# Moving four pieces of work in a two-layer hybrid backbone, and ordering the whole program by a timeline

## The chip, the core and the metric

The kernel runs on one core of a Trainium2 chip. The core has a matrix engine (TensorE, PE in the rows), a vector engine (VectorE, DVE), a scalar engine (ScalarE, ACT), a general engine (GpSimd, POOL) and a queue that issues transfers (SyncE, SP). Each engine works through its own list of instructions in the order in which it was written; the lists meet only through waits on each other and on transfers (DMA). The metric is the time of one execution on the device, in microseconds (us).

## The reference

Two layers act on 1024 latent tokens and 256 context tokens of width 1024, all in fp32. Each layer is

```
h   = modulate(rms_norm(x), shift, scale)
aq,ak,av, bq,bk,bv, cx,cg = split(h @ W_in)       # three head groups
ya  = differential_attention(aq, ak, av)          # 4 heads, two softmax maps each
yb  = window_attention(bq, bk, bv, sink)          # 6 heads, window 128
yc  = bidirectional_RG_LRU(cx) * gelu(cg)         # width 384
x   = x + gate * (concat(ya, yb, yc) @ W_out)
h   = modulate(rms_norm(x), shift, scale)
x   = x + gate * (gelu-gated dwconv MLP(h) @ W_down)   # D_FF = 2816
```

The LRU part runs, for each of three groups of 128 channels and for both directions, a four-tap convolution along the tokens, two gate products with a block-diagonal matrix, a few pointwise functions (tanh, exp, sqrt) and a linear recurrence over all 1280 tokens; both directions are added and multiplied with the gated branch. Only the latent tokens of the last layer are the output.

## The kernel before, in words

A product in fp32 is made of three fast matmuls: each operand is split into a high part (`hi`, a copy on ACT, L184) and a low part (`lo`, a subtraction on DVE or POOL, L187), and high times high, high times low and low times high are added up in one bank of PE's accumulator memory. So every operand of a product has passed ACT and then DVE or POOL before PE can use it.

A layer has three phases. `phase_a` makes the projections of all three head groups, in three rounds j = 0, 1, 2. In each it makes query and key tiles (qkv_ps, with norm and rotation on DVE and POOL, transposed through PE as qk_t) or value tiles, and one third of the LRU: cx_ps, then in `lru` for each direction the convolution (L562, L569), the gates (gate_ps, L578, L579), exp, tanh and sqrt (L583, L584, L587), the pointwise products (L585, L588 on DVE, L586, L590 on POOL) and the recurrence as two scans (L593, L594 or L597, L599), and then in `lru_gate` the sum of both directions (L608), gelu on cg_ps (L614) and their product (L618). `phase_b` is the two attentions (sw for window, da for differential). `phase_c` is the output projection, the second norm, the feed-forward up (`up`, u_ps) and down (`down_steps`, d_ps and dc_ps).

The up products go by a scheme with fewer products: sums of quarters of the operands (s1 to s4, made in `norm_ops`, L1250 to L1264) take the place of some quarters. A product runs over four parts kk of its operand, each a high and a low tile (s_x, s_z). The down products work likewise, in steps: `prep` makes the sums of a product (d_s, d_t on POOL, L1342) and their splits (d_ah, d_al, d_b), and `split_ctx` splits the context operand (four pairs of 128x256, the low parts on POOL). The last two of the 22 slices of the down product are done apart, by `down` (L1735 to L1737), with operands from `load_u` in the last layer. In layer 0 this remainder is run by `tail`, in front of the `phase_a` of layer 1: it reads the residual (xt) back from memory, where `down_steps` stored it (xp), adds its products and makes the norm. This is called the seam. `weights` loads and splits the two weight tiles (w) that it needs.

The program falls into basic blocks: `phase_a` of layer 0, then `phase_b` and `phase_c` of layer 0, then the seam with `phase_a` of layer 1, then the rest of layer 1. Each engine ends a block's list before it begins the next one's. Within a block a scheduler puts each engine's list in order, by a model of when each instruction could start, and keeps dependences; only the seam block was ordered with the finer model, that follows a simulated timeline.

Of the kernel before, what the change touches and what calls it, by code (L numbers as in the profile page):

```python
# [11 lines left out]
F32 = mybir.dt.float32  # L12
F32R = mybir.dt.float32r
AF = mybir.ActivationFunctionType
ALU = mybir.AluOpType
# [155 lines left out]
class Build:  # L171
# [9 lines left out]


    def hi(self, out, in_):
        self.nc.scalar.activation(out, in_, AF.Copy)  # L184

    def lo(self, out, in_, hi, eng=None):
        (eng or self.nc.vector).tensor_tensor(out, in_, hi.bitcast(F32), ALU.subtract)  # L187

    def weight(self, src, n=1024):
        nc = self.nc  # L190
# [988 lines left out]
    def norm_ops(self, xt, am, bm, accs, f_tile, bank, ops, early, outs):  # L1179
# [13 lines left out]
        def unit(name, t, c=0):  # L1193
            p = t[:, c:c + 512], t[:, c + 512:c + 1024]
            ops[name].append(p)
            return p

        def split(p, v, eng):
            self.hi(p[0], v)
            self.lo(p[1], v, p[0], eng)  # L1200
# [51 lines left out]
        for kk in range(4):  # L1252
            s3 = v21[kk]
            nc.vector.tensor_tensor(s3, v11[kk], s3, ALU.subtract)
            split(unit("s3", (wa, wb)[kk // 2], 1024 * (kk % 2)), s3, nc.vector)
        ops["s2"].append(None)
        ops["s4"].append(None)
        for kk in range(4):
# [20 lines left out]
    def down_steps(self, xt, f_tile, bank):  # L1279
# [165 lines left out]
        load_ctx(0)  # L1445
        prep(0)
        prep(1)
        split_ctx()
        if steps > 1:
            load_ctx(1)  # L1450
        g = 0
        for s in range(steps):
            mine = [p for t, p in seq if t == s]
            for i, p in enumerate(mine):
                prep(g + 2)
                g += 1
                if p != "c":
                    product(s, p)
                if not self.last:

                    for q in {1: ("p1",), len(mine) - 1: ("c",)}.get(i, ()) + ((p,) if p in ("p2", "p3") else ()):
                        context(s, q)
                if s + 1 == steps:
                    for n in {"p2": ("x12",), "p5": ("x22",), "p7": ("x21",)}.get(p, ()):
                        spread(n)
                    for n in {"p2": ("x11",), "p7": ("x22",), "p3": ("x12",), "p4": ("x21",)}.get(p, ()):
                        store(n)
            if s + 1 < steps:
                split_ctx()
                if s + 2 < steps:  # L1470
                    load_ctx(s + 2)
# [3 lines left out]
    def phase_c(self):  # L1475
# [3 lines left out]
        with ExitStack() as st:  # L1479
# [65 lines left out]

            def product(ps, w, a, new, wts):
                (wh, wl), aa = wts[w], ops[a]
                for kk in range(4):
                    s = slice(P * kk, P * kk + P)
                    h, lo = aa[kk]  # L1550
                    nc.tensor.matmul(ps, wh[:, s], h, start=new and kk == 0, stop=False, skip_group_check=not new)  # L1551
                    nc.tensor.matmul(ps, wh[:, s], lo, start=False, stop=False, skip_group_check=not new)  # L1552
                    nc.tensor.matmul(ps, wl[:, s], h, start=False, stop=kk == 3, skip_group_check=not new)  # L1553

            def context(ps, w, new, wts):
                hh, hl = hc
# [151 lines left out]
            def load_u(f):  # L1708
                h, lo = self.h_tile("uh"), self.h_tile("ul")
                nc.sync.dma_start(lo[:, :n_tok].bitcast(F32), self.ud[f][:, :n_tok])  # L1710
                self.hi(h[:, :n_tok], lo[:, :n_tok].bitcast(F32))
                self.lo(lo[:, :n_tok], lo[:, :n_tok].bitcast(F32), h[:, :n_tok])
                return h, lo

            def down(fs, us, ds, end=False):
# [34 lines left out]
            if self.last:  # L1750
                ds = weights()
                down([NF - 2, NF - 1], [load_u(f) for f in (NF - 2, NF - 1)], ds)
            else:
                us = []
                for f in (NF - 2, NF - 1):
                    h, lo = f_tile("uh", F32R), f_tile("ul", F32R)
                    nc.sync.dma_start(lo.bitcast(F32), self.ud[f])
                    self.hi(h, lo.bitcast(F32))
                    self.lo(lo, lo.bitcast(F32), h)
                    us.append((h, lo))  # L1760
                stack = st.pop_all()

                def tail():
                    mods, self.mods = self.mods, self.modl[l]
                    ds = weights()
                    for j in range(KC):
                        xt[j] = self.x_tile(f"xt{j}") if j < KC - 1 else self.z_tile("xt7")[:, :T]
                    for o, n in CH:
                        for j in range(KC):
                            nc.sync.dma_start(xt[j][:, o:o + n], self.xp[j][:, o:o + n])  # L1770
                    down([NF - 2, NF - 1], us, ds, True)
                    self.mods = mods
                    stack.close()
                    del self.s5

                self.tail = tail
                return
# [26 lines left out]
```

## Time and profile before

| what | value |
|---|---|
| three timed runs | 3067.39, 3073.74, 3075.61 us; median 3073.74 |
| profiled execution | 3074.54 us, span 3072.8 us, mean granted clock 0.972 |
| PE, matmuls | 2836.2 us busy, 92% of the span |
| PE, weight loads | 2308.8 us, 75% |
| DVE | 2070.9 us, 67% |
| POOL | 1520.2 us, 49% |
| ACT | 1468.6 us, 48% |
| transfers | 349.25 MB, 114 GB/s in the mean |

The span runs from the first to the last instruction of the trace; 1.74 us of the execution lie outside. PE is busy nine tenths of the span, so the mean says little: a stage in which PE never stops and a stage in which it waits for an operand stand side by side. The rows below are read by stage. "Idle before" with an arrow says what ended the idle time of that instruction's engine.

### The profile page before, as it was taken

The numbers are of one execution on the slowest core, as the hardware profiler recorded it, in microseconds if no ns is written. First come the engines' busy times: TensorE is split into PE (matmuls) and PEld (weight loads), VectorE is DVE, ScalarE is ACT, GpSimd is POOL, SyncE is SP. The second block draws the span as 40 slices with busy tenths as digits, with TensorE's granted clock in tenths as the row PEclk, the third lists the DMA queues.
The fourth block names the chain that finished last, engine by engine and source line by source line (L and its number), as shares of the span: only waits on it lengthen the run. The fifth ranks groups of instructions, "written<-read, shape, count | busy, mean of one in ns | idle before, by whom it ended". The sixth has DMA issues, their size and how long they took to land. (4 is left out here: it accounts for less than half of the span.)

```text
span 3072.8 us, 40965 instructions
## 1 busy us (share of the span) xinstructions
PE 2836.2 (92%) x15146; PEld 2308.8 (75%) x15146; DVE 2070.9 (67%) x2879; ACT 1468.6 (48%) x2450; POOL 1520.2 (49%) x1011
## 2 busy tenths in 40 slices
PE   6999898999899999998988899898999799999898
PEld 4798665678688888886877788666777678887776
DVE  6956656884854444457887985757885755556997
ACT  5544467784443433342332554567883444444331
POOL 4746412323554444448561765512323576665971
PEclk9999999999899999998999999999999999999999
DMA  7232627664122111143215331545533122224322
GB/s 254 83 85 82 173 61 248 185 196 172 38 81 76 67 68 67 67 182 113 83 56 192 112 109 52 145 109 168 130 121 131 55 89 83 83 83 158 123 83 83
DMA packets 208280, 349.25 MB, mean 114 GB/s; under 512 B 32720, under 2 KB 112336, under 8 KB 208080
## 3 DMA queue, kind: packets, MB, share of 16 engines
q1 hardware_dynamic: 203472, 331.69, 33.3%
q0 software_dynamic: 4608, 14.95, 2.2%
q8 instruction: 119, 1.95, 0.3%
q14 instruction: 81, 0.66, 0.1%
HBM read 257.19 MB, written 89.39 MB: 113 GB/s over the span
## 5 line engine op out<-in xcount | busy, mean ns | idle before, releaser
L184 ACT ACTIVATE w_r<-w_raw 128x512 fp32r<-128x512 f32 x338 | 212.7, 631 | 451.4 <-PE u_ps L1552 279.7
L1524 POOL TENSOR_TENSOR w_raw<-w_raw 128x512 f32<-128x512 f32 x176 | 249.9, 1425 | 229.3 <-DVE w_r L187 108.5
L187 DVE TENSOR_TENSOR w_r<-w_raw,w_r 128x512 fp32r<-128x512 f32 x206 | 151.3, 737 | 250.2 <-ACT w_r L184 250.1
L1551 PE MATMUL u_ps<-a,w_r 128*128 128x512 f32 x704 | 278.6, 396 | 5.1 <-DVE vb L1639 4.0
L1552 PE MATMUL u_ps<-a,w_r 128*128 128x512 f32 x704 | 277.5, 394 | 1.4 <-DVE a L187 1.2
L1553 PE MATMUL u_ps<-a,w_r 128*128 128x512 f32 x704 | 276.3, 392 | 0.0
L187 POOL TENSOR_TENSOR w_r<-w_raw,w_r 128x512 fp32r<-128x512 f32 x132 | 190.2, 1441 | 122.7 <-ACT w_r L184 117.5
L1403 PE MATMUL d_ps<-d_ah,d_b 128*128 128x512 f32 x560 | 225.2, 403 | 22.5 <-DVE xd L1380 12.3
L1404 PE MATMUL d_ps<-d_al,d_b 128*128 128x512 f32 x560 | 223.9, 400 | 6.2 <-DVE d_al L187 6.2
L946 DVE TENSOR_REDUCE da_sm<-da_s 128x1 f32<-128x1280 f32 (+1 forms) x144 | 194.9, 1367 | 43.6 <-PE da_s L936 42.7
L1405 PE MATMUL d_ps<-d_ah,d_b 128*128 128x512 f32 x560 | 223.3, 399 | 0.6 <-DVE d_b L187 0.6
L187 POOL TENSOR_TENSOR w<-raw,w 128x1024 fp32r<-128x1024 f32 (+2 forms) x62 | 141.1, 2283 | 144.1 <-ACT w L184 135.1
L953 ACT ACTIVATE da_e<-da_s,da_sm 128x1280 f32<-128x1280 f32 (+1 forms) x144 | 177.6, 1235 | 22.9 <-DVE da_sm L946 21.2
L1551 PEld LDWEIGHTS u_ps<-a,w_r 128*128 128x128 f32 x704 | 133.9, 190 | 34.6 <-DVE vb L1639 5.5
L1090 POOL TENSOR_TENSOR oy_x<-oy_x,oy_z 128x426 f32<-128x426 f32 (+3 forms) x48 | 52.1, 1086 | 216.3 <-ACT oy_z L1088 193.7
L1552 PEld LDWEIGHTS u_ps<-a,w_r 128*128 128x128 f32 x704 | 133.9, 190 | 29.5 <-DVE a L187 2.1
L1553 PEld LDWEIGHTS u_ps<-a,w_r 128*128 128x128 f32 x704 | 133.6, 190 | 28.8
L1380 DVE SCALAR_TENSOR_TENSOR xd<-d_ps,mods,xd 128x512 f32<-128x512 f32 x200 | 141.0, 739 | 19.7 <-PE d_ps L1405 19.4
L1403 PEld LDWEIGHTS d_ps<-d_ah,d_b 128*128 128x128 f32 x560 | 108.7, 194 | 48.3 <-DVE xd L1380 10.0
L936 PE MATMUL da_s<-dak,daq 96*128 96x512 f32 (+1 forms) x400 | 123.0, 395 | 13.7 <-ACT da_e L953 13.3
L1639 DVE TENSOR_TENSOR vb<-u_ps,vb 128x512 f32<-128x512 f32 x96 | 66.0, 688 | 99.2 <-PE u_ps L1553 90.5
L1551 PE MATMUL u_ps<-s_x,w_r 128*128 128x512 f32 x308 | 122.0, 396 | 10.1 <-ACT s_x L184 10.1
(349 smaller groups left out, 8616.3 us busy)
## 6 DMA issues: line engine op xcount, KB each, us to landing
wmod<-in_wmod SPq DMA_DIRECT2D x96, 512.0 KB, 6.5
w_raw<-in_wu SPq DMA_DIRECT2D x44, 1024.0 KB, 5.4
d_w<-in_wd SPq DMA_DIRECT2D x40, 512.0 KB, 3.9
d_a<-ud SPq DMA_DIRECT2D x40, 512.0 KB, 4.6
ud<-conv SPq DMA_DIRECT2D x22, 640.0 KB, 2.9
ud<-conv SPq DMA_DIRECT2D x22, 512.0 KB, 2.6
raw<-in_wg SPq DMA_DIRECT2D x16, 512.0 KB, 4.1
dak<-qk_da POOLq DMA_DIRECT2D x48, 160.0 KB, 4.6
```

What stands on the lines that cost most here:

```text
L184: self.nc.scalar.activation(out, in_, AF.Copy)
L187: (eng or self.nc.vector).tensor_tensor(out, in_, hi.bitcast(F32), ALU.subtract)
L946: nc.vector.tensor_reduce(st["sm"][:, mi:mi + 1], st["s"][mi][:, :b["nkc"]], AX.X, ALU.max, negate=True)
L953: nc.scalar.activation(e[:, :nkc], st["s"][mi][:, :nkc], AF.Exp, bias=st["sm"][:, mi:mi + 1], accum_out=b["s0"][:, ti, u["hd"], mi:mi + 1])
L1380: nc.vector.scalar_tensor_tensor(x, ps, gate, x, ALU.mult, ALU.add)
L1403: nc.tensor.matmul(ps, bh[:, w], ah[:, m], start=on is None and k == 0, stop=False, **kw)
L1404: nc.tensor.matmul(ps, bh[:, w], al[:, m], start=False, stop=False, **kw)
L1405: nc.tensor.matmul(ps, bl[:, w], ah[:, m], start=False, stop=k == 1, **kw)
L1524: sub = lambda o, a, b, op=ALU.subtract: nc.gpsimd.tensor_tensor(o, a, b, op)
L1551: nc.tensor.matmul(ps, wh[:, s], h, start=new and kk == 0, stop=False, skip_group_check=not new)
L1552: nc.tensor.matmul(ps, wh[:, s], lo, start=False, stop=False, skip_group_check=not new)
L1553: nc.tensor.matmul(ps, wl[:, s], h, start=False, stop=kk == 3, skip_group_check=not new)
```

## The change

Four pieces of work are moved, and the whole program is ordered by the finer model, not only the seam block.

- Seam weights: `ds = weights()`, two weight loads and their splits, leaves `tail` and is called at the end of `phase_c` of layer 0, so it lies one block earlier.
- s2 parts: in the last layer the sums s2 and s4 and their splits are written in another order, the part kk = 0 late; `product` takes s2 and s4 in the order kk = 1, 2, 3, 0 in both layers.
- Last splits: the two splits of `load_u` are kept in the order of the program, so they are not put ahead of what is written before them.
- Context split: in the first step of layer 0's down products, `split_ctx` and the next load of the context come after the sums of the third product, not after the second.

```diff
+        if self.last:
+            ...
+            s2(0)
+            s4(0)
+            s2(1)
+            put("s2", 1, nc.vector)
+            s2(2)
+            put("s2", 2, nc.vector)
+            s4(1)
+            s2(3)
+            put("s2", 3, nc.vector)
+            s4(2)
+            put("s2", 0, nc.vector)
+            s4(3)
+            put("s4", 1, nc.gpsimd)
+            put("s4", 2, nc.vector)
+            put("s4", 3, nc.gpsimd)
+            put("s4", 0, nc.vector, self.z_tile("s_z", F32R))
+            return None
...
         prep(1)
-        split_ctx()
-        if steps > 1:
-            load_ctx(1)
         g = 0
         for s in range(steps):
...
                 prep(g + 2)
+                if g == 0:
+                    split_ctx()
+                    if steps > 1:
+                        load_ctx(1)
...
-                for kk in range(4):
+                for i in range(4):
+                    kk = (i + 1) % 4 if a in ("s2", "s4") else i
...
-                self.hi(h[:, :n_tok], lo[:, :n_tok].bitcast(F32))
-                self.lo(lo[:, :n_tok], lo[:, :n_tok].bitcast(F32), h[:, :n_tok])
+                tc.keep_in_program_order(self.hi(h[:, :n_tok], lo[:, :n_tok].bitcast(F32)))
+                tc.keep_in_program_order(self.lo(lo[:, :n_tok], lo[:, :n_tok].bitcast(F32), h[:, :n_tok]))
...
+                ds = weights()
                 stack = st.pop_all()
                 def tail():
                     mods, self.mods = self.mods, self.modl[l]
-                    ds = weights()
...
-    with tile.TileContext(nc) as tc:
+    with tile.TileContext(nc, schedule_with_timeline_sim=True) as tc:
```

The numbers of instructions on each engine stay as they were, but for one or two. In the following extracts a row is line, operation, output and inputs, and shape; the changed kernel's line numbers are some 35 to 39 higher.

POOL at the start of layer 0's down products, before: d_al are the four low parts of the context split, d_t and d_s sums for the products to come, d_b low parts of the weights.

```order
L187 TENSOR_TENSOR d_b<-d_t_11539,d_b 128x1024
L1342 TENSOR_TENSOR d_s_11535<-d_a_11553,d_a_11555 128x1024
L187 TENSOR_TENSOR d_al<-d_a_11553,d_ah 128x256
L187 TENSOR_TENSOR d_al<-d_a_11555,d_ah 128x256
L187 TENSOR_TENSOR d_al<-d_a_11554,d_ah 128x256
L187 TENSOR_TENSOR d_al<-d_a_11556,d_ah 128x256
L1342 TENSOR_TENSOR d_t_11538<-d_t_11539,d_w 128x1024
L1342 TENSOR_TENSOR d_t_11540<-d_w,d_t_11538 128x1024
L1342 TENSOR_TENSOR d_s_11533<-d_a_11555,d_a_11556 128x1024
```

The same place on POOL in the changed kernel:

```order
L187 TENSOR_TENSOR d_b<-d_t_11539,d_b 128x1024
L1377 TENSOR_TENSOR d_s_11535<-d_a_11553,d_a_11555 128x1024
L187 TENSOR_TENSOR d_al<-d_a_11553,d_ah 128x256
L187 TENSOR_TENSOR d_al<-d_a_11555,d_ah 128x256
L1377 TENSOR_TENSOR d_t_11538<-d_t_11539,d_w 128x1024
L187 TENSOR_TENSOR d_al<-d_a_11554,d_ah 128x256
L1377 TENSOR_TENSOR d_t_11540<-d_w,d_t_11538 128x1024
L187 TENSOR_TENSOR d_al<-d_a_11556,d_ah 128x256
L1377 TENSOR_TENSOR d_s_11533<-d_a_11555,d_a_11556 128x1024
```

One d_t now stands between the second and the third context split, and the next one between the third and the fourth; d_s_11533 comes in the same place, behind all of them.

ACT at the end of the program, before: uh are the high parts of the last two slices, w the weights for them, d_ah and d_b high parts for the last down products.

```order
L184 ACTIVATE uh<-ul 128x1024
L184 ACTIVATE d_ah<-d_a_22834 128x1024
L184 ACTIVATE d_b<-d_w 128x1024
L184 ACTIVATE d_b<-d_t_22817 128x1024
L184 ACTIVATE d_ah<-d_s_22813 128x1024
L184 ACTIVATE uh<-ul 128x1024
L184 ACTIVATE d_ah<-d_s_22815 128x1024
L184 ACTIVATE d_b<-d_t_22819 128x1024
L184 ACTIVATE d_b<-d_w 128x1024
L184 ACTIVATE d_ah<-d_s_22816 128x1024
L184 ACTIVATE w<-raw 128x1024
```

The end of ACT's list in the changed kernel:

```order
L184 ACTIVATE d_ah<-d_s_22813 128x1024
L184 ACTIVATE d_b<-d_t_22819 128x1024
L184 ACTIVATE d_ah<-d_s_22815 128x1024
L184 ACTIVATE w<-raw 128x1024
L184 ACTIVATE d_b<-d_w 128x1024
L184 ACTIVATE d_ah<-d_s_22816 128x1024
L184 ACTIVATE d_b<-d_t_22820 128x1024
L184 ACTIVATE d_ah<-d_a_22836 128x1024
L184 ACTIVATE w<-raw 128x1024
L184 ACTIVATE uh<-ul 128x1024 x2
```

Both uh are now the last two instructions of ACT; the two low parts ul stand on DVE behind all xd of `down_steps`.

DVE at the end of the seam block (layer 1's `phase_a`), before: qa and qv belong to query and key tiles, tr is the LRU's output, sw_sm the first work of the window attention.

```order
L694 TENSOR_TENSOR qa<-qa,qr 128x256 x2
L187 TENSOR_TENSOR qa<-qk_t,qb 128x512
L187 TENSOR_TENSOR qa<-qk_t,qb 128x256
L618 TENSOR_TENSOR tr<-tr 128x1024
L187 TENSOR_TENSOR qa<-qk_t,qb 128x256
L278 UNCONDITIONAL_BRANCH
L875 TENSOR_REDUCE sw_sm<-sw_s 128x1
```

The same place in the changed kernel:

```order
L589 SCALAR_TENSOR_TENSOR ti<-ti,xc 128x1280
L569 SCALAR_TENSOR_TENSOR xc<-cx,prm_119,xc 128x1021
L585 SCALAR_TENSOR_TENSOR av<-av,tr 128x1280
L569 SCALAR_TENSOR_TENSOR xc<-cx,prm_119,xc 128x253
L588 SCALAR_TENSOR_TENSOR tr<-av,tr 128x1280
L593 SCALAR_TENSOR_TENSOR tr<-av,ti 128x256
L594 SCALAR_TENSOR_TENSOR tr<-av,tr,ti 128x1024
...
L597 SCALAR_TENSOR_TENSOR tr<-av,ti 128x256
L599 SCALAR_TENSOR_TENSOR tr<-av,tr,ti 128x1024
L618 TENSOR_TENSOR tr<-tr 128x1024
L278 UNCONDITIONAL_BRANCH
```

Ahead of these rows stand both directions' convolutions; between L594 and L597 stand L589, L585 and L588 of the second direction. Before, this group's convolutions and scans stood a dozen rows and more higher up, between the query and key tiles. On PE the twelve gate matmuls of the group are now the last ones of the block, behind all qkv_ps, qk_t and cg_ps; before, they stood between the qkv_ps.

## Rows read from the trace of the kernel before

**Rows 1.** Busy time by stretch; then granted clock (PEclk), DMA share, GB/s.

```profile
2480.00:2810.00 330.00, 330.00 (x1445) 270.98 (x1444) 168.19 (x207) 142.59 (x222) 218.09 (x150) 1.00 0.26 90
2411.00:2421.00 10.00, 8.49 (x25) 6.43 (x26) 4.05 (x6) 2.14 (x5) 3.24 (x4) 0.65 0.28 105
3007.00:3017.00 10.00, 9.61 (x33) 7.76 (x34) 10.00 (x12) 4.92 (x6) 2.44 (x1) 0.75 0.16 52
```

**Rows 2.** Waits of PE: line, for whom, us in total, times, longest us.

```profile
PE dc_ps L1425 <- DVE xd L1380: 26.3, 14, 6.7
PE qk_t L699 <- DVE qa L694: 19.5, 10, 6.3
...
PE d_ps L1403 <- DVE xd L1380: 12.3, 6, 5.9
PE u_ps L1551 <- ACT s_x L184: 10.1, 1, 10.1
PE n_bc L399 <- POOL nr L396: 8.5, 5, 5.3
...
PE cx_ps L427 <- ACT cx L554: 5.9, 1, 5.9
PE d_ps L1735 <- ACT w L184: 5.9, 1, 5.9
PE qk_t L699 <- DVE qa L187: 4.4, 1, 4.4
```

**Rows 3.** Timeline, POOL at the context split: start, us, instruction, [idle before].

```profile
1381.51 2.95 POOL L187 TENSOR_TENSOR d_al<-d_a,d_ah 128x256 fp32r<-128x256 f32 x2 [6.25 <-PE d_ps L1405]
...
1389.23 2.34 POOL L1342 TENSOR_TENSOR d_s<-d_a,d_a 128x1024 f32<-128x1024 f32 x1
```

**Rows 4.** Timeline, DVE at the context split.

```profile
1392.69 2.28 DVE L187 TENSOR_TENSOR d_al<-d_s,d_ah 128x1024 fp32r<-128x1024 f32 x1 [5.97 <-ACT d_ah L184]
1394.89 0.47 DVE L1380 SCALAR_TENSOR_TENSOR xd<-dc_ps,mods,xd 128x256 f32<-128x256 f32 x1
```

**Rows 5.** Timeline, DVE at layer 1's sums for the up products.

```profile
2384.26 6.90 DVE L1250 SCALAR_TENSOR_TENSOR xr<-xr,bs,xr 128x512 f32<-128x512 f32 x4
...
2412.57 0.68 DVE L187 TENSOR_TENSOR s_x<-s_x,s_x 128x512 fp32r<-128x512 f32 x1
```

**Rows 6.** Timeline, DVE at the seam.

```profile
1674.94 4.04 DVE L1782 SCALAR_TENSOR_TENSOR xt<-d_ps,mods,xt 128x512 f32<-128x512 f32 x6 [12.88 <-DMA xt<-xp]
```

**Rows 7.** Timeline, ACT near the end.

```profile
3004.30 1.06 ACT L184 ACTIVATE uh<-ul 128x1024 fp32r<-128x1024 f32 x1 [8.11 <-DMA ul<-ud]
```

**Rows 8.** Timeline, DVE near the end.

```profile
3045.74 5.35 DVE L1380 SCALAR_TENSOR_TENSOR xd<-d_ps,mods,xd 128x512 f32<-128x512 f32 x8
```

**Rows 9.** Timeline, PE, first matmul of the last product.

```profile
3046.89 0.39 PE L1735 MATMUL d_ps<-uh,w 128*128 128x512 f32 x1
```

**Rows 10.** Timeline, DVE, LRU of the last group in layer 1.

```profile
1903.02 0.95 DVE L562 TENSOR_SCALAR xc<-cx,prm 128x1280 f32<-128x1280 f32 x1 [16.57 <-ACT cx L554]
...
1922.77 2.87 DVE L569 SCALAR_TENSOR_TENSOR xc<-cx,prm,xc 128x1023 f32<-128x1023 f32 x3
...
1929.01 1.48 DVE L585 SCALAR_TENSOR_TENSOR av<-av,tr 128x1280 f32<-128x1280 f32 x1
...
1943.09 2.34 DVE L594 TENSOR_TENSOR_SCAN tr<-av,tr,ti 128x1024 f32<-128x1024 f32 x1
...
1961.91 2.34 DVE L599 TENSOR_TENSOR_SCAN tr<-av,tr,ti 128x1024 f32<-128x1024 f32 x1
```

**Rows 11.** Timeline, ACT, LRU of the first group in layer 1.

```profile
1773.23 1.28 ACT L583 ACT_TABLE_LOAD   x1
1774.53 1.46 ACT L583 ACTIVATE av<-tr,lruc 128x1280 f32<-128x1280 f32 x1
```

**Rows 12.** Timeline, POOL, LRU of the last group in layer 1.

```profile
1937.02 3.37 POOL L590 TENSOR_TENSOR ti<-ti,tr 128x1280 f32<-128x1280 f32 x1
```

**Rows 13.** Timeline, PE, gates of the first group in layer 1.

```profile
1765.54 1.59 PE L578 MATMUL gate_ps<-xc,lw 128*128 128x428 f32 x4
```

More of the change, by code (lines that the diff above doesn't have):

```diff
@@ L183, in hi @@
     def hi(self, out, in_):
-        self.nc.scalar.activation(out, in_, AF.Copy)
+        return self.nc.scalar.activation(out, in_, AF.Copy)
     def lo(self, out, in_, hi, eng=None):
-        (eng or self.nc.vector).tensor_tensor(out, in_, hi.bitcast(F32), ALU.subtract)
+        return (eng or self.nc.vector).tensor_tensor(out, in_, hi.bitcast(F32), ALU.subtract)
     def weight(self, src, n=1024):
@@ L1255, in norm_ops, with s2, s4, put @@
             split(unit("s3", (wa, wb)[kk // 2], 1024 * (kk % 2)), s3, nc.vector)
+        if self.last:
+            ops["s2"], ops["s4"] = [None] * 4, [None] * 4
+            raw = [(v11[kk], v12[kk]) if kk else (sx[:, 0:512], sx[:, 512:1024]) for kk in range(4)]
+            def s2(kk):
+                nc.vector.scalar_tensor_tensor(raw[kk][0], v22[kk], bm[:, 2 * kk, 0:1], v11[kk], ALU.subtract,
+                                               ALU.subtract)
+            def s4(kk):
+                nc.vector.scalar_tensor_tensor(raw[kk][1], v12[kk], bm[:, 2 * kk + 1, 0:1], raw[kk][0], ALU.add,
+                                               ALU.subtract)
+            def put(n, kk, eng, t=None):
+                t = t or slot()
+                ops[n][kk] = t[:, 0:512], t[:, 512:1024]
+                split(ops[n][kk], raw[kk][n == "s4"], eng)
+            s2(0)
[15 more added lines that the diff above has]
+            return None
         ops["s2"].append(None)
@@ L1547, in product @@
                 (wh, wl), aa = wts[w], ops[a]
-                for kk in range(4):
+                for i in range(4):
+                    kk = (i + 1) % 4 if a in ("s2", "s4") else i
                     s = slice(P * kk, P * kk + P)
                     h, lo = aa[kk]
-                    nc.tensor.matmul(ps, wh[:, s], h, start=new and kk == 0, stop=False, skip_group_check=not new)
+                    nc.tensor.matmul(ps, wh[:, s], h, start=new and i == 0, stop=False, skip_group_check=not new)
                     nc.tensor.matmul(ps, wh[:, s], lo, start=False, stop=False, skip_group_check=not new)
-                    nc.tensor.matmul(ps, wl[:, s], h, start=False, stop=kk == 3, skip_group_check=not new)
+                    nc.tensor.matmul(ps, wl[:, s], h, start=False, stop=i == 3, skip_group_check=not new)
             def context(ps, w, new, wts):
```

## The prediction

> **What bounds the kernel now.** Read the stages first, then the waits, then the instructions around each wait. In the stage table [rows 1] TensorE (PE) is busy 330.00 of 330.00 us of the steady feed-forward at a granted clock of 1.00: nothing can be won there, so the time lies where PE stands still. The list of waits [rows 2] says where, with how often and the longest: a few single waits of 4 to 10 us, and swarms of short ones that nothing in the change is aimed at. Each long wait is paid twice. Behind the 10.1 us wait for s_x the clock is 0.65 over ten microseconds, behind the 5.9 us wait for the last xd it is 0.75 [rows 1]: means over stretches at its two levels, 1.2 and 2.4 GHz, worth 3.5 and 2.5 us. I charge 2.5 us of half clock to every removed or new wait of 4 us or more.
>
> The sum is made against the profiled run, 3074.54 us (span 3072.8, 1.74 around it); the median of the three times is 3073.74, so the total is taken 0.8 lower at the end.
>
> **The change part by part.** The counts of instructions stay; only places move.
>
> *Context split.* Before, VectorE (DVE) stands 5.97 us in front of a d_al, with the xd that frees PE's bank behind it [rows 4], and PE waits 6.7 us. That d_al waits for ACT's hi part of a d_s that POOL starts at 1389.23, behind four context splits and two d_t [rows 3]. Now DVE has that xd ahead, and PE has 24 matmuls of the next product ahead of the context ones. All of it would be 6.7 + 2.5 = 9.2 us. But the d_s itself moves up little: POOL put one d_t into the 6.25 us in which it stood [rows 3], so its chain is 2.4 us (one d_t) earlier, no more, and the next products need it. Bounds 2.4 and 9.2; I take 5, between, since PE's banks come free at once and only the second half of the relief hangs on POOL.
>
> *Last layer's s2.* Before, DVE's chain from the first sum at 2384.26 to the low part that PE needs at 2412.57 is 31 instructions [rows 5], and PE waits 10.1 us [rows 2]. Now the first low part needed (kk=1) is the 25th, and twelve matmuls of another product stand in front of it. A place is 0.68 us beside an idle POOL and 6.90/4 = 1.73 us in the stretch at 2384 [rows 5]. Six places are 4.1 or 10.4 us. The upper end is cut by the fourth part (kk=0), which is 33rd now, and by the wait itself. Bounds 3 and 12.6 (10.1 + 2.5); I take 6, nearer to 0.68, which holds at the place in question.
> The Trainium skill ("SBUF — State Buffer", Who interferes with whom) says that a VectorE instruction with two SBUF inputs and a GpSimd instruction that reads SBUF exclude one another. The two durations in this row group agree with that; it speaks against handing s4 parts to POOL here: two such splits, each holding one DVE instruction for the difference of the two durations, would take 2 us off this term.
>
> *Norm of layer 0.* The 5.3 us wait for nr [rows 2] goes down if DVE's nv of the third chunk moves ahead of the s1 sums, as it does now; other waits of the same 25 us stay. Bounds 0 and 7.8 (5.3 + 2.5); I take 4.
>
> *Seam weights.* PE's wait of 5.9 us for w [rows 2] goes. What is late next is DVE: its first residual of the seam starts at 1674.94, after waiting 12.88 us for xt from DMA [rows 6], and that load follows the stores, not the weights. SP issues two weight loads fewer ahead of it, about 0.9 us. PE fills its banks early and stops there. Bounds -1 (the two loads now stand between stores) and 8.4; I take 1: this transfer hides the gain.
>
> *Last splits.* ACT stands 8.11 us for the DMA of ul, with a d_ah behind it [rows 7]; PE waits 5.9 us. With both uh at the end of ACT's list this goes: 5.9 + 2.5 = 8.4. The price is at the other end: both ul now stand behind the last sixteen-odd xd on DVE. Eight of these take 5.35 us and end at 3051.1 [rows 8], 4.2 us after PE began its last product at 3046.9 [rows 9]. Two ul of 1.2 us follow; PE has twelve matmuls (2.7 us) that need no ul, so it waits some 2.7 us, 4 with the clock. Bounds -2 and 8.4; I take 4.5.
>
> *The order of layer 1's projections.* This is the adverse part. In the last of the three head groups the whole recurrent (LRU) chain now stands behind all projections: the block ends on PE with the twelve gate matmuls, on DVE with both directions' convolutions and scans. No engine passes from one block to the next out of order, so window attention's first reduction on DVE waits for it. From the last cx: a convolution of 6 us (0.95 and three pairs, 2.87 for three of the six [rows 10]); PE's other 43 matmuls of 330/1445 = 0.228 us [rows 1] and four short ones last longer, about 11 us in all; four gate outputs 2 us (each a third of exp's 1280 columns), a table load 1.28, exp 1.46, two more outputs 1, tanh like exp [rows 11]: 18.5. Then 1.48 on DVE, the same again on POOL, 1.48 on DVE, 3 on POOL (3.4 beside a busy DVE), scans 0.6 + 2.34 [rows 10, 12]: 29. The second direction is ready on ACT by then and adds 1.48 twice, a sqrt like exp, 1.48, 3 and 3: 41; the sum of directions, gelu and product, fewer columns of the same kinds, 4.5: about 45 us. PE has 11 us of matmuls, 12 gates of 0.4 [rows 13] and 2 us of scores to lay beside it. It stands 28 us, 30.5 with the clock, where before it stood 6.3 for qa [rows 2], 8.8 with the clock: a loss of 21.5.
> Against that, LRU work no longer stands between the first groups' rope instructions: the waits of 5.9 (cx) and 4.4 us (qa L187) [rows 2] go, 15.3 with the clock. Net loss 6. Its ends: both directions took from 1903.02 to 1964.25 before, 61 us with other work between [rows 10], which instead of 41 makes the loss 26, and 41 if the two waits stay; if the chain is covered as before, it is a gain of 15.
> The Trainium skill ("ScalarE: Activation LUTs", What ACT_TABLE_LOAD costs) counts a drain of 1.38 us on top of each load. The trace disagrees: exp starts 0.02 us after the load's end [rows 11]. By the page five loads in this chain would cost 7 us more, and the net loss would be 13.
>
> *Everything else* is put in order anew, by some rows up and down. In the full stage it can only lose; in the attention stages the waits are short. I take 0, bounds -8 and +8.
>
> Sum: 5 + 6 + 4 + 1 + 4.5 - 6 = 14.5 off 3074.5 gives 3060; less 0.8 by the median, 3059. I say 3060.
>
> **The rivals.** *The late LRU chain wins.* For: every engine ends the block with it, and nothing of the next block can start. Against: without rope instructions between, it should be faster than the 61 us of before. With these 61 us and the two early waits staying, 41 is lost and 20.5 won: 3094 at the far end, 3087 where one of the two waits stays. It decides for slower once the block costs more than 30 us net. *The waits only move.* PE waits for POOL at the split, for DVE at the end, and for the late s2 part; each edit gives its lower third: 8 us, less 6 of the block: 3072. For it speaks that DVE is busy without a break from 3007 to 3017 [rows 1]. The seam is the part that does not do what it says in any of these. *The chain is covered.* If PE's products of the last group run late enough beside it, the block gains 15 and the edits 20.5: 3038. Against: the gates are its very last matmuls.
>
> **How the numbers follow.** Forecast 0.43, late chain 0.20, waits move 0.22, covered 0.15. The forecast's own range is 3048 to 3072, from the bounds of its terms partly cancelling. The range that takes in the others is 3036 to 3089. What a measurement of this kernel can tell from no change is 0.3%, 9 us: below 3064.5 is faster, above 3083 slower. Faster: 0.36 of the forecast, 0.15 covered, 0.05 of moving waits, 0.56; slower: 0.15 of the late chain and 0.03 of the rest, 0.18; within: 0.26.
>
> **What would show it.** Right: at the start of layer 1's window attention PE stands 20 us or more, with DVE's last scan and the LRU product just before; the waits for s_x, cx, ACT's w and the last xd are gone or under 3 us; DVE's first seam residual still waits for xt until about as long after the last store as now; a wait of 2 to 4 us for ul before the last product. Wrong: a wait under 10 us at the head of that attention (the chain is covered), or new waits over 5 us in the steady stages, which no term here holds.

## The result: 74 us slower, and where

| | median of the runs shown | lowest to highest | runs |
|---|---|---|---|
| before | 3071.0 us | 3067.39 to 3075.61 | 4 |
| after | 3145.16 us | 3142.57 to 3146.17 | 4 |

The ratio is 1.0239, with a 95% interval of 1.0222 to 1.0257. The forecast was 3060 (3036 to 3089): wrong in sign, and the time lies 56 us outside the range. The profiled run of after took 3146.17 us, its span is 3144.3.

The first thing to make is a table of stages. A stage here goes from the start of its first matmul to the start of the next stage's first matmul, read from the two traces and from those of four experiments told below (E1: the four moves, coarser model; E2: finer model alone; E3: three moves without the seam weights; E4: the seam weights alone). The last stage ends with its last matmul. A profiled run is one run and not the median: E2's lies 10 us above it, E7's 5 and E12's 9 below. Microseconds:

| stage | before | after | E1 | E2 | E3 | E4 |
|---|---|---|---|---|---|---|
| window attention 0 | 126.6 | 142.3 | 125.8 | 141.5 | 126.4 | 126.7 |
| differential attention 0 | 242.9 | 269.6 | 242.4 | 270.1 | 241.4 | 242.5 |
| up products 0 | 574.3 | 580.9 | 574.0 | 582.9 | 574.0 | 574.1 |
| down products 0 | 298.3 | 268.6 | 286.4 | 279.2 | 290.7 | 292.5 |
| seam | 33.1 | 34.7 | 35.9 | 33.3 | 33.6 | 35.3 |
| layer 1's projections | 281.2 | 322.9 | 319.4 | 278.3 | 280.0 | 317.3 |
| window attention 1 | 109.3 | 119.4 | 113.1 | 122.3 | 109.3 | 113.0 |
| differential attention 1 | 205.1 | 211.6 | 204.6 | 213.2 | 206.8 | 205.7 |
| up products 1 | 452.7 | 451.8 | 453.9 | 458.4 | 452.4 | 453.4 |
| down products 1 | 251.5 | 245.6 | 246.0 | 246.0 | 246.5 | 250.7 |

Between before and after two things cost and one pays: the four attention stages +59 us, layer 1's projections +42, layer 0's down products -30. What is left out of the table (layer 0's projections, the output projections) makes -1 together. A wait for a stage's first operand lies, by this division, in the stage ahead: so the 5.9 us for which PE stands for a seam weight [rows 2] count to layer 0's down products, before:

```profile
1667.12 0.80 PE L1735 MATMUL d_ps<-uh,w 128*128 128x512 f32 x1 [5.87 <-ACT w L184]
```

The same stages by busy time. Columns: the stretch and its length, then busy time and number of instructions of PE, PEld, DVE, ACT and POOL, the granted clock, DMA share, GB/s. Before: window attention 0, differential attention 0, down products 0, layer 1's projections.

```profile
341.50:468.00 126.50, 112.18 (x706) 81.63 (x707) 71.61 (x188) 77.01 (x197) 18.24 (x44) 0.96 0.45 112
468.00:710.90 242.90, 223.49 (x1713) 161.70 (x1711) 188.32 (x288) 190.27 (x368) 76.92 (x64) 0.99 0.62 200
1368.80:1667.10 298.30, 262.63 (x1322) 221.55 (x1320) 238.85 (x290) 85.94 (x100) 172.95 (x78) 0.95 0.31 101
1700.20:1981.50 281.30, 262.34 (x1243) 222.36 (x1243) 218.09 (x284) 141.47 (x209) 180.22 (x104) 0.96 0.34 93
```

After, the same four:

```profile
339.70:482.00 142.30, 120.41 (x703) 81.70 (x703) 71.95 (x189) 73.75 (x194) 18.19 (x44) 0.96 0.42 102
482.00:751.50 269.50, 233.68 (x1692) 167.42 (x1691) 196.71 (x291) 189.34 (x368) 73.33 (x63) 0.96 0.59 186
1418.30:1686.90 268.60, 257.40 (x1323) 218.13 (x1322) 244.04 (x287) 86.19 (x100) 185.53 (x80) 0.98 0.34 110
1721.60:2044.40 322.80, 271.72 (x1242) 225.24 (x1242) 204.13 (x282) 140.70 (x204) 157.94 (x102) 0.91 0.30 80
```

In the projections the same matmuls take PE 9.4 us more at a clock of 0.91 in place of 0.96, and PE stands 51.1 us in place of 19.0. In the down products PE stands 11.2 us in place of 35.7. In the two attention stages it is some of each: 7.6 and 16.4 us more standing, 8.2 and 10.2 more busy.

The longer waits of PE in layer 1's projections, after (line, for whom, us in total, times, longest), which answer to the cx and qa waits of [rows 2]:

```profile
PE qkv_ps L636 <- ACT w L184: 10.6, 2, 9.1
PE qk_t L699 <- DVE qa L694: 6.8, 3, 3.5
PE qkv_ps L636 <- DVE qb L685: 5.8, 3, 4.6
PE qkv_ps L636 <- DVE xt L1821: 5.6, 1, 5.6
PE gate_ps L578 <- issue: 5.6, 1, 5.6
```

The wait for cx is gone, but three others of 4.6 to 9.1 us (for w, for qb and before the gates) stand in the stage, and the longest is just past this list, before window attention's first score. The wait for xt ends at the stage's first matmul, so it belongs to the seam; there it was 2.4 us before. The timeline of PE at that point (start, us, instruction, idle before), then of DVE and ACT:

```profile
2007.55 4.98 PE L578 MATMUL gate_ps<-xc,lw 128*128 128x428 f32 x12
2018.09 3.18 PE L578 MATMUL gate_ps<-xc,lw 128*128 128x428 f32 x4 [5.56 <-issue]
2022.68 4.94 PE L578 MATMUL gate_ps<-xc,lw 128*128 128x426 f32 x8 [1.40 <-ACT tr L579]
2044.45 0.80 PE L866 MATMUL sw_s<-swk,swq 128*128 128x256 f32 x2 [16.83 <-ACT tr L614]
```

```profile
1998.09 0.95 DVE L562 TENSOR_SCALAR xc<-cx,prm 128x1280 f32<-128x1280 f32 x1 [9.13 <-ACT cx L554]
...
2038.44 2.35 DVE L599 TENSOR_TENSOR_SCAN tr<-av,tr,ti 128x1024 f32<-128x1024 f32 x1
```

```profile
2011.51 1.28 ACT L583 ACT_TABLE_LOAD   x1
2012.81 1.45 ACT L583 ACTIVATE av<-tr,lruc 128x1280 f32<-128x1280 f32 x1
...
2043.31 1.09 ACT L614 ACTIVATE tr<-cg_ps 128x512 f32<-128x512 f32 x2 [8.88 <-POOL tr L608]
```

The recurrent chain runs from 1998.09 on DVE to 2044.4 on ACT, 46.3 us. PE still has the last projections up to 2007.55 and behind them nothing but gates: 5.56 + 1.40 + 16.83 = 23.8 us of standing. The price goes on after the wait. Two stretches of after, the second of which is the beginning of window attention:

```profile
2012.50:2044.40 31.90, 8.16 (x13) 3.30 (x12) 16.69 (x13) 18.90 (x21) 10.78 (x5) 0.61 0.41 96
2044.40:2057.30 12.90, 9.59 (x39) 9.03 (x40) 6.43 (x18) 5.77 (x13) 2.75 (x7) 0.51 0.97 264
```

Window attention 1 begins at a clock of 0.51, that is at 1.2 GHz for nearly all of these 13 us, and is 4 us longer than before also where this wait comes with the coarser model (E1 and E4 above).

### The profile page after: what moved, and what is told of

Read it like the earlier page. It is cut to its first block, busy times and chain, and to the rows that moved or that the text cites. A ratio compares the mean times of both kernels' runs of the same rounds, so it can differ in the third digit from the quotient of the medians.

```text
span 3144.3 us, 40854 instructions
## 1 busy us (share of the span) xinstructions
PE 2875.9 (91%) x15146; PEld 2323.2 (74%) x15146; DVE 2091.9 (67%) x2878; ACT 1463.4 (47%) x2449; POOL 1511.7 (48%) x1012
## 5 line engine op out<-in xcount | busy, mean ns | idle before, releaser
L1560 POOL TENSOR_TENSOR w_raw<-w_raw 128x512 f32<-128x512 f32 x176 | 241.8, 1375 | 255.6 <-DMA w_raw<-in_wu 118.9
L187 DVE TENSOR_TENSOR w_r<-w_raw,w_r 128x512 fp32r<-128x512 f32 x206 | 180.2, 876 | 184.8 <-ACT w_r L184 184.7
L187 POOL TENSOR_TENSOR w_r<-w_raw,w_r 128x512 fp32r<-128x512 f32 x132 | 197.3, 1495 | 99.8 <-ACT w_r L184 94.0
L1438 PE MATMUL d_ps<-d_ah,d_b 128*128 128x512 f32 x560 | 221.1, 401 | 14.1 <-DVE xd L1415 7.1
L1440 PE MATMUL d_ps<-d_ah,d_b 128*128 128x512 f32 x560 | 219.6, 400 | 0.2 <-DVE d_b L187 0.2
L187 POOL TENSOR_TENSOR w<-raw,w 128x1024 fp32r<-128x1024 f32 (+2 forms) x62 | 134.7, 2180 | 174.6 <-ACT w L184 140.7
L936 PE MATMUL da_s<-dak,daq 96*128 96x512 f32 (+1 forms) x400 | 110.7, 385 | 25.5 <-ACT da_e L953 23.5
L1439 PEld LDWEIGHTS d_ps<-d_al,d_b 128*128 128x128 f32 x560 | 108.7, 194 | 32.0 <-DVE d_al L187 10.5
```

Of the source, the lines that this page charges most:

```text
L187: return (eng or self.nc.vector).tensor_tensor(out, in_, hi.bitcast(F32), ALU.subtract)
L1438: nc.tensor.matmul(ps, bh[:, w], ah[:, m], start=on is None and k == 0, stop=False, **kw)
L1439: nc.tensor.matmul(ps, bh[:, w], al[:, m], start=False, stop=False, **kw)
L1440: nc.tensor.matmul(ps, bl[:, w], ah[:, m], start=False, stop=k == 1, **kw)
L1560: sub = lambda o, a, b, op=ALU.subtract: nc.gpsimd.tensor_tensor(o, a, b, op)
```

## The experiments

All ratios are to the kernel before, run on the same chip beside them, with 95% intervals.

### E1 to E4: taking the change apart

E1, all of the change but the finer model:

```diff
-    with tile.TileContext(nc, schedule_with_timeline_sim=True) as tc:
+    with tile.TileContext(nc) as tc:
```

> The changed kernel without the finer model for the whole program: the four moves alone. Theory: two separate causes. (a) The finer model's order of the blocks with attention costs the 59 us that the four attention stages are longer in the changed kernel (16 and 27 in layer 0, 10 and 6 in layer 1). (b) Taking the two seam weights out of the seam block turns that block's order over and costs the 37 us that seam and layer 1's projections are longer together. Here (a) is gone and (b) stays: attention stages as before within 4 us, seam block 30 to 40 us longer. The 24 us that layer 0's down products gained come either from the moved context split (then 3071 + 37 - 24 - 8 = 3076) or from the finer order (then about 3098). Rival: everything that is lost comes from the finer model, the seam block too: then 3035 to 3050.

Measured: 3098.79 us (3094.99 to 3104.47), ratio 1.0081 (1.0064 to 1.0098).

E2, the kernel before with that one line of the finer model and nothing moved. The line gives the model to `phase_b` and `phase_c` of both layers; layer 0's `phase_a` stood in a block with it already, as the seam block did, since one `with` around `phase_a` serves both layers.

> The kernel before with the finer model for the whole program and none of the four moves. Theory: the attention stages are 50 to 65 us longer, the seam block as before within 8 us; layer 0's down products shorter by some 20 us if the finer order is what gained there, as before if it was the context split. So 3071 + 59 - 20 = 3110, or 3130. Rival (the finer model loses everywhere, the seam block too): 3150 or more.

Measured: 3117.97 us (3114.43 to 3127.95), ratio 1.0149 (1.0132 to 1.0167).

E3, E1 with `ds = weights()` back in `tail`:

> Three of the four moves (s2 parts, last splits, context split), seam weights where they were, old model outside the seam block. Theory: faster than before by what the moves take from PE's waits: s2 6, last splits 4 to 6, context split 5 (only its own wait) to 24 (all of the down stage's gain): 3036 to 3056. Rival (the moves only shift waits): within 9 us of 3071.

Measured: 3063.46 us (3060.26 to 3065.94), ratio 0.9966 (0.9953 to 0.9980). The total lies in the rival's range, 7 us above that of the theory.

E4, the kernel before with only the seam weights moved:

```diff
+                ds = weights()
                 stack = st.pop_all()
                 def tail():
                     mods, self.mods = self.mods, self.modl[l]
-                    ds = weights()
```

> The kernel before with only the two seam weight loads and splits moved one block earlier. Theory: 30 to 40 us slower, nearly all between the seam and the first window scores of layer 1, with a wait of PE of 15 us or more at the end of that block; the wait of 5.9 us for w at the seam gone. About 3105. Rival (the seam block's loss needs the finer model): 3071 within 9 us, or 5 faster.

Measured: 3110.22 us (3107.35 to 3110.98), ratio 1.0117 (1.0102 to 1.0132).

The parts add up. Against before on this chip (3073.86) they are -10 (E3), +36 (E4) and +44 (E2), sum +70; E3 and E4 together are E1's +25, and the whole change is +74 on its chip. The stage table says where each acts. The finer model costs the attention stages 63 us and the up products 14, and pays 19 and 5.5 in the down products; these stages, from a run 10 us above E2's median, add up to some 9 us more than the +44. The seam weights cost the projections 36 us and window attention 1 another 4. They pay 5.8 in layer 0's down products: that is the wait for w at the end of this stage, which goes. The three other moves pay 7.6 and 5.0 in the two down products, and nothing where s2 is (up products 1: 452.7 and 452.4).

### Why two early weights cost 36 us in a stage that doesn't use them

The weight tiles of the kernel share six slots (WT_BUFS = 6). In the built program of before, the seam block's tiles go round all six addresses; in E1 and E4 two addresses hold the seam weights, made ahead of the block, and the block's other tiles go round four. A head group's products need four weight tiles, so the recurrent projection's weight has to wait until these are done, and its matmuls come behind the group's products. Places of the first of them in PE's order of the seam block (1352 matmuls), and the stage's length:

| kernel | slots left | recurrent products begin at | projections, us |
|---|---|---|---|
| before | 6 | 258, 571, 950 | 281.2 |
| E6: one early weight | 5 | 285, 596, 976 | 288.6 |
| E4: two early weights | 4 | 428, 812, 1212 | 317.3 |
| E5: late weights, two slots held | 4 | 428, 812, 1212 | 319.0 |
| E12: two early, first group's recurrent weight first | 4 | 172, 812, 1212 | 319.8 |

E5 is the test that tells lost slots from early loads: the weights are loaded late as ever, but two tiles that nobody needs are held.

```diff
+                hold = [self.wt_tile("hold") for _ in range(2)]
+                for t in hold:
+                    nc.gpsimd.memset(t[:, 0:1].bitcast(F32), 0.0)
                 stack = st.pop_all()
...
                     down([NF - 2, NF - 1], us, ds, True)
+                    nc.gpsimd.tensor_tensor(self.s5("hx")[:, 0:1], hold[0][:, 0:1].bitcast(F32), hold[1][:, 0:1].bitcast(F32), ALU.add)
```

> The kernel before, seam weights loaded late as ever, but two tiles of the weight tag are made ahead of the layer-1 block and read at the end of the seam, so that two of the six weight slots are taken all block long. Theory (what costs 36 us is the two lost slots, by which the weights of the recurrent projections come after all products of their head group): the loss is there without any early load, 3100 to 3115 us; from the first product of layer 1's projections to the first score of its window attention some 317 us in place of 281; layer 0's down products as before (298). Rival (the early loads themselves do it, in the load queue or between the stores): 3068 to 3082, projections 278 to 286.

Measured: 3117.91 us (3112.55 to 3121.92), ratio 1.0141 (1.0124 to 1.0158), 3 us above the range that the theory gave. The loss is there without any early load, and so is its mark, the wait of the first score for the last recurrent gate. Two of PE's waits from 1700 to 2019 us of E5:

```profile
PE sw_s L866 <- ACT tr L614: 16.6, 1, 16.6
PE qkv_ps L636 <- ACT w L184: 13.0, 3, 9.4
```

Layer 0's down products (298.5) and the seam (33.1) are those of before, as the theory said; the rival is out.

E6 takes one slot only:

```diff
+                d0 = self.weight(self.a["wd"][l, NF - 2])
                 stack = st.pop_all()
...
-                    ds = weights()
+                    ds = [d0, self.weight(self.a["wd"][l, NF - 1])]
```

> The kernel before with only one of the two seam weights loaded early: five slots are left to the block. Theory (slots): five are enough for the four weights of a group's products and one of the recurrent projections, so these stay early: 3064 to 3075 us, projections 279 to 286, and most of the 6 us that the early weights save in layer 0's down products (292 to 296 in place of 298). Rival (the loss grows with each early weight): half of 36 us, 3085 to 3098, projections 295 to 305.

Measured: 3077.51 us (3075.80 to 3079.35), ratio 1.0015 (1.0005 to 1.0024): between the two expectations for the whole, nearer the first. With five slots the recurrent products stay early and the wait at the block's end doesn't come; the stage still loses 7.4 us (expected: up to 5), and the one early weight pays 5.7 in layer 0's down products, as much as two did: the wait at the end of that stage goes with the first of them.

E10 and E11 leave the block around the seam and layer 1's projections out, so that a tile from outside can give its slot back when its last reader is done; the work then stands in one block with the phases before and behind it. E10 has all four moves, E11 the seam weights back in `tail`; both use the coarser model.

```diff
-        with self.tc.block(schedule_with_timeline_sim=True):
+        with ExitStack() as blk:
+            if not l:
+                blk.enter_context(self.tc.block(schedule_with_timeline_sim=True))
```

> All four moves, the coarser model, and no block around the seam and layer 1's projections: a tile from outside gives its slot back when its last reader is done, and not at a block's end. Both seam weights are early. TensorE then has the products of the recurrent projections early again in each head group (places 268, 572 and 944 of 1352, where the four moves with the block have 428, 812 and 1212). Theory (the block holds the slots, and the late recurrent chain is the loss): from the first product of layer 1's projections to the first score 278 to 295 us in place of 319, the whole 3050 to 3075. Rival (two early weights cost it in any case): 312 us or more, 3088 to 3105.

> The three moves without the seam weights, and no block around the seam and layer 1's projections: the control of the run beside it, which differs in the early seam weights alone. TensorE has the recurrent products at the same places in both. Theory (slots): layer 1's projections within 4 us of the run beside it, the whole 0 to 8 us slower than that, by layer 0's down products; against the three moves with the block it shows what the finer model is worth in the projections, -5 to +15 us. Rival (early weights cost by themselves): 30 us or more faster than the run beside it.

Measured: 3084.18 us (3079.79 to 3088.39), ratio 1.0029 (1.0019 to 1.0040), and 3084.26 us (3080.48 to 3087.73), ratio 1.0032 (1.0022 to 1.0042). Layer 1's projections from the first product to the first score, E10, then E11:

```profile
1708.20:1998.40 290.20, 267.25 (x1231) 220.87 (x1231) 183.77 (x256) 125.01 (x180) 150.60 (x92) 0.95 0.33 92
```

```profile
1711.00:2001.00 290.00, 266.42 (x1239) 220.74 (x1239) 185.30 (x257) 124.79 (x179) 149.90 (x91) 0.95 0.34 93
```

Without the block two early weights cost nothing in the projections (290.1 in both) and pay nothing in the whole. Projections and their difference came out as expected, but E10's total is 9 us above its range, for a reason that no theory held: the seam is 54.5 and 55.5 us long in place of 33 to 36. So the block and the finer model in it, which these runs give up together, are worth 31 us in seam and projections (314.3 before, 345.6 in E11). The early weights are not the fault by themselves, but their slots in a block that keeps them; and to give up the block brings back 11 us of that (E1: 355.3 for seam and projections, E10: 344.6), not 36.

E12 asks for the first group's recurrent weight ahead of the group's four (two lines of `phase_a` in layer 1 exchanged, all four moves, coarser model):

```diff
-                ws = [self.qkv_weight("wg2", kk) for kk in range(4)]
                 wx = self.weight(self.a["wc"][l, 0])
+                ws = [self.qkv_weight("wg2", kk) for kk in range(4)]
```

> The four moves with the coarser model, and in layer 1 the recurrent projections' first weight asked for ahead of the four of the first head group: only the first group's recurrent products come early (places 172 to 283 of 1352), the other two stay late (812 and 1212). Theory (the loss is the last group's chain, which nothing covers, with the half clock behind it): little comes back, projections 309 to 319 us, in all 3088 to 3100. Rival (each group loses a third): 303 to 308 us, 3078 to 3088.

Measured: 3101.88 us (3092.53 to 3103.69), ratio 1.0078 (1.0060 to 1.0096). The projections take 319.8 us: the first group's chain, moved early, gives nothing back, and the 16.6 us before the first score stay. That agrees with the theory that the last group's chain is what costs; it is no proof for the whole 36 us, since the early start may have been paid for by other waits (5.7 us of cg_ps for qb is new here).

### The finer model in attention and in the down products

E7 puts window attention alone, of both layers, into a block that the finer model orders:

```diff
-                self.sw(pss, v, loaded)
+                with tc.block(schedule_with_timeline_sim=True):
+                    self.sw(pss, v, loaded)
```

> The kernel before with window attention alone (both layers) in a block of its own that the finer model orders; in its steady part TensorE's order is then that of the run with the finer model alone. Theory (it is this order that costs the attention stages their time): layer 0's window attention 138 to 146 us in place of 126.6, layer 1's 118 to 126 in place of 109.3, in all 3092 to 3106. Rival (the loss comes from outside, loads that come later, or blocks of the whole program): under 131 and 113, 3070 to 3082.

Measured: 3144.55 us (3139.34 to 3145.49), ratio 1.0230 (1.0215 to 1.0245): more than either expectation. Window attention takes 151.9 and 135.1 us in place of 126.6 and 109.3, and the stages behind it lose 11 and 9 (254.3 and 214.0). The block's two ends have a price of their own, so the totals don't separate order from block. The steady part does: from 384.6 to 474.6 us E7 runs at one matmul in 183 ns, E2 (372 to 462) at one in 180, where before (370 to 445) took 162, each the stretch divided by the matmuls recorded in it. TensorE's order there is the same in E7 and E2. So the order of the finer model costs about a tenth of the speed, and no late load is needed for that.

What in the order costs it, the waits show in part. PE in window attention 0, before:

```profile
PE sw_t L846 <- ACT sw_p L878: 9.5, 9, 3.6
PE sw_t L846 <- ACT sw_pbs L830: 2.2, 2, 1.6
PE sw_t L846 <- ACT sw_w L857: 0.4, 1, 0.4
```

After:

```profile
PE sw_s L866 <- DMA swq<-qk_sw: 7.8, 2, 5.8
PE sw_t L846 <- ACT sw_pbs L830: 5.2, 9, 0.7
PE sw_t L846 <- ACT sw_p L878: 3.6, 1, 3.6
PE sw_t L846 <- ACT sw_w L857: 2.3, 10, 0.3
```

Two patterns changed. At the start PE now stands for a query load, up to 5.8 us, which it never did before; the first 30 us hold 93 matmuls at a clock of 0.83, before 138 at 0.89:

```profile
339.70:369.70 30.00, 18.46 (x93) 13.72 (x94) 13.77 (x33) 11.47 (x27) 10.09 (x21) 0.83 1.03 224
```

```profile
341.50:371.50 30.00, 24.15 (x138) 18.63 (x139) 15.65 (x40) 15.88 (x37) 4.40 (x10) 0.89 0.84 227
```

And in every round transposes (sw_t) stand in rows of eight and four behind a PSUM tile that ACT is still emptying, where before one to five scores lay between rows of mostly three or four of them. Before, then after:

```profile
374.44 0.42 PE L866 MATMUL sw_s<-swk,swq 128*128 128x384 f32 x1
374.70 0.49 PE L846 MATMUL sw_t<-cst_all,sw_p 128*128 128x128 f32 x3
374.95 0.42 PE L866 MATMUL sw_s<-swk,swq 128*128 128x384 f32 x1
```

```profile
395.14 1.25 PE L846 MATMUL sw_t<-cst_all,sw_p 128*128 128x128 f32 x8 [0.58 <-ACT sw_pbs L830]
396.54 0.66 PE L846 MATMUL sw_t<-cst_all,sw_p 128*128 128x128 f32 x4 [0.15 <-ACT sw_w L857]
```

The full lists sum to 20 us of waits, before 14: 6 of the 16 us. PE's busy time grew by 8 for the same matmuls; part of it is the clock of the first 30 us, and how far the rest is short pauses that the modelled ends of matmuls hide was not settled. In differential attention 0 the wait of da_s for ACT's da_e went from 5.1 us in 7 to 13.7 in 19:

```profile
PE da_s L936 <- ACT da_e L953: 13.7, 19, 1.4
```

No experiment isolates that stage.

E9 is the trial of a better kernel: the three moves of E3, one early weight as in E6, and the finer model for layer 0's down products alone.

```diff
-            self.down_steps(xt, f_tile, bank)
+            if self.last:
+                self.down_steps(xt, f_tile, bank)
+            else:
+                with tc.block(schedule_with_timeline_sim=True):
+                    self.down_steps(xt, f_tile, bank)
```

> The three moves that paid together (s2, context split, last splits), one seam weight early, and the finer model for layer 0's down products alone, in a block of its own. Theory (the finer model's order wins in the down products: 279 and 269 us in place of 298 with it; the rest is as in the three moves alone): 3040 to 3056, layer 0's down products 270 to 283, attention and projections as in the three moves alone. Rival (that gain needs the order of what stands around it, and the end of a block costs a drain): 3060 to 3074, down products 288 to 298.

Measured: 3075.52 us (3068.82 to 3078.18), ratio 1.0007 (0.9997 to 1.0016): no gain, and above both expectations. The down products fall to 283.9 us (E3: 290.7). Each has a wait for a seam weight at its end, 6.0 us in E3 and 8.7 here, in spite of the early weight:

```profile
1662.63 0.79 PE L1778 MATMUL d_ps<-uh,w 128*128 128x512 f32 x1 [8.73 <-ACT w L184]
```

Without it they take 284.7 and 275.2, so about half of the 19 us that the finer model pays there is the order inside the stage. PE's waits of dc_ps for xd, 22.1 us in E3, are short:

```profile
PE dc_ps L1460 <- DVE xd L1415: 6.9, 9, 2.1
```

But the stage ahead grows from 574.0 to 584.7. At the block's start PE waits once, in the stretch from 1366 to 1385 us:

```profile
PE d_ps L1438 <- ACT d_b L184: 10.7, 1, 10.7
```

A block can't prepare its first product in the block ahead. The early weight then costs 9 us in the projections, as in E6. Of all kernels run, E3 is the fastest, and faster than both that were compared.

## Why the prediction was wrong, point by point

- *Everything else: 0, bounds -8 and +8.* This is the step that failed most. Attention was said to have short waits, so that a new order could give and take little; the attention stages lost 59 us. The term was taken from the waits of before, which say how much a better order could win. They say nothing of what a worse one can lose, and the order of window and differential attention was not read. The steady feed-forward, said to be able to lose only, lost 7 us in layer 0. Nor did the term hold the 19 us that the finer model won in layer 0's down products; in all it measured -44 (E2) in place of 0.
- *The order of layer 1's projections: -6.* Place and mechanism of its adverse half were right. The chain was worked out at 45 us, it took 46.3 without the last product; PE was to stand 28 us there, it stood 23.8. It stood less because the gates kept it longer: the x4 of [rows 13] was read as four gates, but the twelve are 24 records, and these took 4.98 + 3.18 + 4.94 = 13.1 us in place of 4.8. (The loss of 21.5 is 21.7 by its own terms, 30.5 less 8.8; nothing hangs on it.) The other half failed: 15.3 us were to come back because the recurrent work stood no longer between the first groups' rope instructions. The cx wait and the qa wait of 4.4 us did go, but waits of 9.1 (w) and 4.6 us (qb) came for them; E5, with two slots held, has these too (9.4 and 4.6), so the lost slots bring them. The clock was mis-sized too: 2.5 us for each long wait, where PE's busy time in the stage grew by 9.4 and window attention 1 by 4. Net -42 in place of -6. It was put down to no edit; E4 and E5 show that the seam weights cause it, through the slots.
  The Trainium skill ("ScalarE: Activation LUTs", What ACT_TABLE_LOAD costs) adds a drain of 1.38 us to a load; in after exp starts 0.02 us behind a load's end (2011.51 + 1.28, 2012.81), as before, and the chain came out without it.
- *Rivals.* The late chain wins, at 0.20 and 3087 to 3094, was the nearest, and its condition was met: the block cost more than 30 us net. Its reason was not: it took a chain of 61 us, which was 46.3, and early waits that stayed, which went. Its far end lay outside the stated range already. None spoke of attention or of weight slots.
- *Seam weights: 1.* At its own place the term was nearly right: in E4 PE's wait for w went, 5.8 us, and the wait for xt grew from 2.4 to 6.2, as forecast, so that the seam is 2.2 us longer; 3.6 are left. What the term put at nothing is the slots: moved early, the two weights cost 36 us in the projections and 4 behind them.
- *Context split: 5.* The 6.7 us wait [rows 2] is 4.4 in E3: it is 2.4 us shorter, the lower bound. E3's stage gives 7.6, of which 4.4 is busy time of PE, at a mean clock of 0.98 in place of 0.95. Of the 29.7 us of after 5.9 are the wait for w, and most of the rest is the finer model's (19.1 alone, in E2): PE's wait of dc_ps for xd went from 26.3 us in 14 [rows 2] to 6.7 in 7. E3, then after:

```profile
1390.70 0.58 PE L1460 MATMUL dc_ps<-d_ah,d_b 128*128 128x256 f32 x1 [4.37 <-DVE xd L1415]
```

```profile
PE dc_ps L1460 <- DVE xd L1415: 6.7, 7, 2.3
```

- *s2: 6.* Mis-sized: 0.3 in E3 (up products 1). The wait of 10.13 us became three of 1.16, 0.72 and 4.01 before products of s_x and one of 2.43 for w_r. Over the first 135.4 us of the stage PE stands 3.3 us less than before and is 3.3 us longer busy with the same matmuls, at the same mean clock: a part of the half clock that came while PE stood now comes while it works. Before, then E3:

```profile
2364.60:2500.00 135.40, 115.28 (x483) 90.21 (x482) 98.75 (x123) 58.69 (x93) 75.53 (x51) 0.95 0.17 61
```

```profile
2355.60:2491.00 135.40, 118.62 (x484) 91.73 (x483) 97.74 (x122) 58.58 (x93) 77.67 (x52) 0.95 0.17 61
```

  Two stretches inside these, before while PE stands and E3 while it works:

```profile
2401.00:2411.00 10.00, 0.00 (x0) 0.00 (x0) 10.00 (x13) 4.90 (x8) 4.96 (x3) 0.67 0.00 1
```

```profile
2422.00:2441.00 19.00, 17.20 (x67) 13.58 (x66) 10.61 (x13) 6.31 (x11) 10.51 (x7) 0.89 0.30 116
```

  With the finer model and no edit (E2) the long wait isn't there either: s_x from ACT costs PE 3.0 us.

- *Norm of layer 0: 4.* Failed. The 5.3 us wait of n_bc for nr [rows 2] is 5.85 in after.

```profile
867.36 0.69 PE L399 MATMUL n_bc<-cst_all,nr 128*128 128x128 f32 x2 [5.85 <-POOL nr L396]
```

- *Last splits: 4.5.* Right: 5.0 in E3. The 5.9 of after can't be put down to it, since the finer model alone gives 5.5 there (E2). In E3 the xd wait of 5.9 us is 1.7 and ul costs 1.7 us ahead of the last product, forecast 2.7:

```profile
3034.73 0.51 PE L1776 MATMUL d_ps<-ul,w 128*128 128x512 f32 x1 [1.72 <-DVE ul L187]
```

- *The sign.* The edits that were aimed at a wait summed to 20.5 in the forecast; the three of E3, 15.5 of these, gave 10. The forecast lost on what the other two parts, the finer model and the seam weights, did in stages that the edits don't name.
- *The signs.* The wait before the first score was to be 20 us or more and is 16.8, and it ends with gelu on ACT, ahead of the last product. In after no wait of 2 us or more stands before the last product for ul. New waits over 5 us in the steady stages were named as a sign of being wrong. New ones came, 9.1 us for w in layer 1's projections and 5.8 us for a query load in window attention 0, though both near a stage's start.

## What to carry to other kernels

A switch that puts the whole program in order anew is to be priced stage by stage, and a stage with short waits is one with something to lose: its order has to be read like any edit. A load that is moved ahead of a block takes its buffer with it; count the slots that the block has left and what is queued for them before asking what the load hides. And an order that is good for one stage does not move into a block of its own for nothing: the block's start cost 11 us here.

## What the runs showed of the hardware

After a wait of 16.8 us TensorE's granted clock was 0.51 over the first 13 us of work (2044.4 to 2057.3 above), which is 1.2 GHz nearly throughout; behind a wait of 10 us of before ten microseconds were at 0.65 [rows 1]. With 9.59 us of busy PE in these 13, the half clock cost some 5 us by estimate; the stage is 3.8 and 3.7 us longer in E1 and E4, where the same wait is 16.9 us. That is more than the 2.5 that the forecast charged to any long wait.
